# Start addresses of tiles: small tiles in a pool of their own, large tiles and rows on multiples of 64 bytes

## The chip, the cores and the metric

The kernel runs on one core of a Trainium2 chip. The metric is the device time of one execution in microseconds (us), as the median of several runs. The profile shows one execution, taken with the hardware profiler.

The engines are called as in the profile: PE is the matmul engine, with PEld for its loading of weights; DVE does elementwise work and reductions; ACT does activations and copies; POOL and SP complete them. SP's queue issues nearly all transfers here.

## The reference

An encoder trunk of two layers over 256 tokens of width 1024, in float32. Each layer adds three branches to x; each branch is normalised and modulated by shift, scale and gate that come from a condition vector c.

```python
c_act = jax.nn.silu(c)
for i in range(DEPTH):                                   # DEPTH = 2
    mod = (c_act @ mod_w[i] + mod_b[i])[:, None, :]      # 1024 -> 9 * 1024
    sh0, sc0, g0, sh1, sc1, g1, sh2, sc2, g2 = jnp.split(mod, N_MOD, axis=-1)
    h = modulate(rms_norm(x, norm_g[i, 0]), sh0, sc0)
    x = x + 0.5 * g0 * swiglu(h, ffn_w_gu[i, 0], ffn_w_down[i, 0])
    h = modulate(rms_norm(x, norm_g[i, 1]), sh1, sc1)
    y = pool_mixer(h, ...) if i == 0 else diff_attention(h, ...)
    x = x + g1 * y
    h = modulate(rms_norm(x, norm_g[i, 2]), sh2, sc2)
    x = x + 0.5 * g2 * swiglu(h, ffn_w_gu[i, 1], ffn_w_down[i, 1])
return rms_norm(x, final_g)
```

`swiglu` is `(silu(h @ Wg) * (h @ Wu)) @ Wd` with an inner width of 2816. The pooling mixer subtracts each token from its window's mean and multiplies by four matrices of 256 x 256. The attention has 8 heads with two softmaxes each, of which one is subtracted from the other.

## The kernel before

The tokens lie along the free dimension: `xT`, the running x, is 128 partitions x 8 rows x 256 tokens. A matmul has 128 x 128 weights, and 256 tokens stream past them.

Float32 products are made of three matmuls of the single-pass type `float32r`. Each operand is split into `hi`, its rounded value, and `lo`, what is left; the product is hi*hi + hi*lo + lo*hi (`prod3`, lines 333 to 335; `mm_deferred`, lines 431 to 433, does the same for the columns that are not normalised yet). The activations have such pairs in `xh`/`xl` (x times its scale), `hh`/`hl` (normalised), and `ah`/`al`, the two halves of `ahl` (inner activations of the feed-forward, values and outputs of the attention).

All weights come as a stream of 312 units of 128 x 1024 or 128 x 768 values. `split_unit` (line 304) takes for each a tile `raw` of 5 buffers, issues its load on SP's queue (line 310), lets ACT round it into `hi` (line 313) and DVE subtract it into `lo` (line 314); those have 6 buffers each. `prefetch` keeps five units ahead of the matmuls. A unit is issued again only when its buffers are free, so the matmuls pull the stream along.

Beside it runs the modulation, c times `mod_w`: 144 loads of 128 x 1024 into `u` (6 buffers, SP's queue), each followed by one multiply with sum on DVE (line 272). A list (`UP`, `DOWN`) says in which part of which feed-forward each of these steps is done; `Background.tick` spreads them over the units.

The stages follow one another: feed-forward, pooling mixer, feed-forward, then in layer 1 feed-forward, attention (its steps in an order written out by hand, `SCHED`), feed-forward, and the final norm. A tile framework orders each engine's instructions by priority and sets the semaphores.

Tiles come from pools. A pool hands out places in the order in which its tags are first asked for, and rounds each place up to a multiple of 32 bytes of a partition; pools lie one behind the other in the order in which they are made: `cpool` (what stays), `rawp`, `hip`, `lop`, `tmp`. Of what stays, in order of place: `ident` and `ones` (512 bytes each), `eps1` (4 bytes), `xT`, `xh`, `xl`, `hh`, `hl`, `ahl`, `cact`, `vecT` (836 bytes), the two `mod` (288 bytes each), `acc`, and some twenty vectors of 4 to 64 bytes. In the built program `ident` begins at byte 16,512 of a partition, `xT` at 17,568, `xh` at 25,760, `hh` at 42,208, `ahl` at 58,592, `acc` at 109,184, the five `raw` from 110,752 on, the six `hi` from 131,232, the six `lo` from 155,808, `u` from 189,632, `t` from 214,208. A row of `xh` has 258 values, or 1,032 bytes: 256 tokens and two columns for the shift, which `shift_cols` (line 409) writes and `shift_of` (line 452) reads back from the product.

`tmp` holds the temporary tiles, large and small: `t`, `u`, `qk`, `pk`, `rope`, `o`, and the tags `tiny`, `tinyw`, `tinyv`, `warm`, `rstdc` of 4 to 16 bytes.

Of the kernel before, what the change touches and what calls it, by code (L numbers as in the profile page):

```python
# [11 lines left out]
F32 = mybir.dt.float32  # L12
F32R = mybir.dt.float32r
# [3 lines left out]
AX = mybir.AxisListType  # L17

P = 128
D = 1024  # L20
KD = D // P
T = 256
NT = T // P
DFF = 2816
KF = DFF // P
EPS = 1e-6
# [36 lines left out]
def weight_units():  # L63

    def block(name, lead, r0, r1, c0, c1):
        return name, (*lead, slice(r0, r1), slice(c0, c1))

    def halves(name, lead, c0):
        yield block(name, lead, 0, 512, c0, c0 + UW)
        yield block(name, lead, 512, 1024, c0, c0 + UW)  # L70

    def ffn(i, s):
        first = 0
        if (i, s) == (0, 0):
            first = EARLY
            for k in range(KD):
                for n in range(2):
                    yield block("ffn_w_gu", (i, s), k * P, (k + 1) * P, n * DFF, n * DFF + EARLY * UW)
        for j in range(first, KF // 2):
            for n in range(2):  # L80
                yield from halves("ffn_w_gu", (i, s), n * DFF + j * UW)
        for dp in range(D // UW):
            for k0, k1 in DOWN_K:
                yield block("ffn_w_down", (i, s), k0 * P, k1 * P, dp * UW, (dp + 1) * UW)

# [5 lines left out]
    for tok in SCHED.split():  # L91
        n, u = tok[0], int(tok[1])
        if n in "qkv":
            yield from halves("diff_w_qkv", (), "qkv".index(n) * D + u * UW)
        elif n in "AB":
# [5 lines left out]
def unit_shape(ix):  # L101

    return (ix[-2].stop - ix[-2].start) // P, ix[-1].stop - ix[-1].start

# [8 lines left out]
def lay_out(inputs):  # L113
# [4 lines left out]
    head = np.concatenate([np.arange(16, 64), np.arange(0, 16), np.arange(64, P)])  # L118
    order = np.concatenate([h * P + head for h in range(2 * HEADS)] + [np.arange(2 * D, 3 * D)])
    w["diff_w_qkv"] = w["diff_w_qkv"][:, order]  # L120
    w["pool_w"] = w["pool_w"].reshape(D, UW)
    w["k_pool"] = consts["k_pool"]
# [20 lines left out]
def trunk(ctx: ExitStack, tc: tile.TileContext, x, c, mod_w, small, weights, diff_lambda, k_rope, out):  # L143
# [3 lines left out]
    cpool = ctx.enter_context(tc.tile_pool(name="cpool", bufs=1))  # L147
    rawp = ctx.enter_context(tc.tile_pool(name="rawp", bufs=RAW_BUFS))
    hip = ctx.enter_context(tc.tile_pool(name="hip", bufs=SPLIT_BUFS))
    lop = ctx.enter_context(tc.tile_pool(name="lop", bufs=SPLIT_BUFS))  # L150
    tmp = ctx.enter_context(tc.tile_pool(name="tmp", bufs=2))
    ps = ctx.enter_context(tc.tile_pool(name="ps", bufs=4, space=bass.MemoryType.PSUM))

    uid = [0]

    def nm(s):
        uid[0] += 1
        return f"{s}_{uid[0]}"

    def const(shape, name, dt=F32):  # L160
        return cpool.tile(shape, dt, tag=name, name=name)

    def psum():
        return ps.tile([P, 512], F32, tag="mm", name=nm("mm"), bufs=4)
# [4 lines left out]
    def psmall():  # L169
        return ps.tile([P, 512], F32, tag="st", name=nm("st"), bufs=2)  # L170
# [2 lines left out]
        return tmp.tile([P, n], F32, tag=tag, name=nm(tag), bufs=bufs)  # L173

    def tiny(n, dt=F32, tag="tiny", bufs=8):
        return tmp.tile([P, n], dt, tag=tag, name=nm(tag), bufs=bufs)

    def tinyw(n, dt=F32):
        return tiny(n, dt, "tinyw", 8)

    def tinyv(n, dt=F32):
        return tiny(n, dt, "tinyv", 6)
# [5 lines left out]


    ident = const([P, P], "ident")  # L190
    make_identity(nc, ident)
    ones = const([P, P], "ones")
    V.memset(ones, 1.0)

    pt = psum()
    for _ in range(WARM):
        PE.matmul(pt[:, :P], ones, ones, start=True, stop=True)

    eps1 = const([P, 1], "eps1")
    V.memset(eps1, 1.0)  # L200

    xT = const([P, KD, T], "xT")
    xh = const([P, KD, T + 2], "xh", F32R)
    xl = const([P, KD, T], "xl", F32R)
    hh = const([P, KD, T], "hh", F32R)
    hl = const([P, KD, T], "hl", F32R)
# [3 lines left out]
    def warm(f, after):  # L210

        S.activation(tiny(1, tag="warm", bufs=1), after, f, scale=0.0, bias=eps1)


    cact = const([P, D], "cact")
    for half in range(2):
# [132 lines left out]
    def newton(y, y0, v, t):  # L349
        V.tensor_tensor(t, y0, y0, ALU.mult)  # L350
        V.scalar_tensor_tensor(t, t, -0.5, v, ALU.mult, ALU.mult)
        V.scalar_tensor_tensor(y, t, 1.5, y0, ALU.add, ALU.mult)
# [27 lines left out]
    def rstd_cols():  # L380

        pt = psmall()
        for q in range(NT):
            PE.matmul(pt[:, q:q + 1], acc[:, q * P:(q + 1) * P], ones[:, 0:1], start=True, stop=True)
        v = tiny(NT)
        V.tensor_scalar(v, pt[:, :NT], 1.0 / D, EPS, ALU.mult, ALU.add)
        y = tmp.tile([P, NT], F32, tag="rstdc", name=nm("rstdc"), bufs=2)
        y0 = tiny(NT)
        S.activation(y0, v, AF.Abs_reciprocal_sqrt)
        newton(y, y0, v, tiny(NT))  # L390
        return y
# [167 lines left out]
    def pool_mixer(nxt):  # L559
# [5 lines left out]
        S.activation(hh[:, :, 0:P], bb, AF.Copy)  # L565
        V.tensor_tensor(hl[:, :, 0:P], bb, hh[:, :, 0:P].bitcast(F32), ALU.subtract)
        rstd = rstd_cols()

        def group(pt, g, q, lh, ll):
# [358 lines left out]
```

## Time and profile before

| | |
|---|---|
| median of 3 runs | 938.18 us (938.16 to 942.18) |
| the profiled execution | 942.75 us, its span 940.9 us |
| mean granted clock of PE | 0.992 |
| matmuls in the span | 7532 |
| read from HBM | 234.86 MB, 251 GB/s over the span |

The profile lists for each engine its busy time; matmuls overlap one another, so the time that one of them costs is read from start to start, in the timeline or by the count in a stretch. The chain of work is followed back from the last instruction: at each step to what released it. "L333" is line 333 of the kernel. A group such as "L335 PE MATMUL mm<-hh,lo" names the tile that is written, then the streamed tile, then the weights; a number such as x992 is its count.

### The profile page before, as it was taken

To read this page: it belongs to the slowest core of one execution; us is meant where nothing else is said; L and a number is where in the kernel's file an instruction comes from. 1 tells how busy PE (TensorE), PEld (TensorE's weight loads), DVE (VectorE), ACT (ScalarE), POOL (GpSimd) and SP (SyncE) were. 2 spreads that over 40 slices of the span, in tenths; PEclk is the share of its full clock that TensorE was granted. 3 is DMA by queue.
4 is the path that set the end of the run, shared out by engine and by line. 5 is a ranking of instruction groups with operands and counts; after the bars stand their busy time and mean duration, and the time that the engine had idled before them with its cause. 6 is when DMAs were issued, how large, how long until landed. Compare 5 with 4: busy or idle time off the path is not lost.

```text
span 940.9 us, 18753 instructions
## 1 busy us (share of the span) xinstructions
PE 911.2 (97%) x7532; PEld 897.5 (95%) x7532; DVE 743.6 (79%) x1211; ACT 505.4 (54%) x771; POOL 0.7 (0%) x6
## 2 busy tenths in 40 slices
PE   7899999899999999999999999999999999999997
PEld 7898889798999999999999999999999999999996
DVE  5868888789999777887988888888888897666451
ACT  5564435445665445455654454557777765444541
POOL 0000000000000000000000000000000000000000
PEclk9999999999999999999999999999999999999998
DMA  8988999888659887898599888855546548655531
GB/s 339 355 301 304 317 335 357 298 313 285 245 192 324 288 282 265 299 317 285 179 356 324 311 304 306 264 194 162 158 132 224 185 154 277 193 182 181 169 122 45
DMA packets 68727, 238.18 MB, mean 253 GB/s; under 512 B 7968, under 2 KB 9248, under 8 KB 68640
## 3 DMA queue, kind: packets, MB, share of 16 engines
q1 hardware_dynamic: 68496, 236.88, 73.8%
q8 instruction: 59, 0.97, 0.4%
q14 instruction: 28, 0.23, 0.1%
q10 hardware_dynamic: 144, 0.11, 0.0%
HBM read 234.86 MB, written 1.05 MB: 251 GB/s over the span
## 4 chain that ended last, share of the span: by engine, by line
PE 72%; DMA 12%; DVE 8%; ACT 4%; issue 3%; SPq 1%; DVEq 0%; ACTq 0%
PE mm L333 18%; PE mm L335 18%; PE mm L334 17%; DMA raw<-in_weights_dram 10%; DVE u L272 3%; DVE lo L314 3%; PE hd L335 3%; PE hd L333 3%; PE hd L334 3%; ACT hi L313 2%; PE mm L431 2%; PE mm L433 2%; PE mm L432 2%; PE hd L644 1%; DMA u<-in_mod_w_dram 1%
## 5 line engine op out<-in xcount | busy, mean ns | idle before, releaser
L313 ACT ACTIVATE hi<-raw 128x1024 fp32r<-128x1024 f32 (+1 forms) x312 | 318.6, 1025 | 339.2 <-PE mm L334 170.0
L314 DVE TENSOR_TENSOR lo<-raw,hi 128x1024 fp32r<-128x1024 f32 (+1 forms) x312 | 366.6, 1181 | 139.7 <-ACT hi L313 137.5
L335 PE MATMUL mm<-hh,lo 128*128 128x256 f32 x992 | 276.6, 281 | 4.4 <-DVE lo L314 4.4
L333 PE MATMUL mm<-hh,hi 128*128 128x256 f32 x992 | 277.7, 281 | 0.1
L334 PE MATMUL mm<-hl,hi 128*128 128x256 f32 x992 | 276.7, 280 | 0.0
L335 PE MATMUL mm<-ahl,lo 128*128 128x256 f32 x768 | 215.1, 280 | 2.2 <-DVE lo L314 2.2
L333 PE MATMUL mm<-ahl,hi 128*128 128x256 f32 x768 | 215.1, 280 | 1.8 <-ACT hi L313 1.8
L334 PE MATMUL mm<-ahl,hi 128*128 128x256 f32 x768 | 214.7, 280 | 0.0
L335 PEld LDWEIGHTS mm<-hh,lo 128*128 128x128 f32 x992 | 185.5, 188 | 6.6 <-DVE lo L314 6.0
L333 PEld LDWEIGHTS mm<-hh,hi 128*128 128x128 f32 x992 | 186.6, 188 | 1.3 <-ACT hh L420 0.4
L334 PEld LDWEIGHTS mm<-hl,hi 128*128 128x128 f32 x992 | 186.6, 188 | 0.0
L272 DVE SCALAR_TENSOR_TENSOR u<-u,cact 128x1024 f32<-128x1024 f32 x144 | 173.9, 1218 | 0.2 <-DMA u<-in_mod_w_dram 0.2
L335 PEld LDWEIGHTS mm<-ahl,lo 128*128 128x128 f32 x768 | 144.1, 188 | 3.4 <-DVE lo L314 3.4
L333 PEld LDWEIGHTS mm<-ahl,hi 128*128 128x128 f32 x768 | 144.2, 188 | 2.5 <-ACT hi L313 2.2
L334 PEld LDWEIGHTS mm<-ahl,hi 128*128 128x128 f32 x768 | 144.2, 188 | 0.0
L333 PE MATMUL hd<-hh,hi 128*128 128x256 f32 x288 | 81.2, 282 | 5.9 <-ACT hi L313 5.9
L335 PE MATMUL hd<-hh,lo 128*128 128x256 f32 x288 | 81.6, 283 | 3.9 <-DVE lo L314 3.9
L334 PE MATMUL hd<-hl,hi 128*128 128x256 f32 x288 | 80.7, 280 | 0.0
L333 PEld LDWEIGHTS hd<-hh,hi 128*128 128x128 f32 x288 | 54.3, 189 | 6.5 <-ACT hi L313 6.5
L335 PEld LDWEIGHTS hd<-hh,lo 128*128 128x128 f32 x288 | 54.3, 188 | 5.2 <-DVE lo L314 5.1
L432 PE MATMUL mm<-xl,hi 128*128 128x256 f32 x208 | 58.8, 285 | 0.0
L433 PE MATMUL mm<-xh,lo 128*128 128x258 f32 x208 | 58.3, 282 | 0.0
(199 smaller groups left out, 1034.7 us busy)
## 6 DMA issues: line engine op xcount, KB each, us to landing
raw<-in_weights_dram SPq DMA_DIRECT2D x264, 512.0 KB, 4.6
u<-in_mod_w_dram SPq DMA_DIRECT2D x144, 512.0 KB, 5.5
raw<-in_weights_dram SPq DMA_DIRECT2D x48, 384.0 KB, 5.0
xT<-in_x_dram SPq DMA_DIRECT2D x2, 512.0 KB, 5.0
out_dram<-u SPq DMA_DIRECT2D x4, 256.0 KB, 2.5
cact<-in_c_dram SPq DMA_DIRECT2D x1, 512.0 KB, 7.1
pk<-qk SPq DMA_DIRECT2D x16, 32.0 KB, 2.9
qk<-pk SPq DMA_DIRECT2D x16, 32.0 KB, 2.0
```

The lines of the kernel that those rows point to most:

```text
L272: return V.scalar_tensor_tensor(raw, raw, 1.0, cact, ALU.mult, ALU.mult, accum_out=out)
L313: S.activation(hi[:, :w], raw[:, :w], AF.Copy)
L314: splits.append(V.tensor_tensor(lo[:, :w], raw[:, :w], hi[:, :w].bitcast(F32), ALU.subtract).ins)
L333: PE.matmul(o, lh, rh, start=start, stop=False, **kw)
L334: PE.matmul(o, lh, rl, start=False, stop=False, **kw)
L335: PE.matmul(o, ll, rh, start=False, stop=stop, **kw)
L431: PE.matmul(o[:, :T + 2], hi[:, kk, cs], xh[:, k, :], start=(k == 0), stop=False)
L432: PE.matmul(o[:, :T], hi[:, kk, cs], xl[:, k, :], start=False, stop=False)
L433: PE.matmul(o[:, :T + 2], lo[:, kk, cs], xh[:, k, :], start=False, stop=(k == KD - 1))
L644: PE.matmul(sc[c2][:, q * T:(q + 1) * T], l[pr, 0, qs], r[pr, 1, :], start=(n == 0), stop=(n == 2))
```

## The change

Tiles whose last dimension is not a multiple of 16 values (64 bytes) move from `cpool` into a new pool `small_p`, which lies behind `tmp`; so do the tags `tiny`, `tinyw`, `tinyv`, `warm` and `rstdc`, which were in `tmp`. They keep their tags and numbers of buffers. `xh` gets rows of 272 values, 1,088 bytes, of which the first 258 are used as before. All instructions stay what they were, with other addresses.

```diff
+LINE = 16
...
     tmp = ctx.enter_context(tc.tile_pool(name="tmp", bufs=2))
+    small_p = ctx.enter_context(tc.tile_pool(name="small_p", bufs=1))
...
     def const(shape, name, dt=F32):
-        return cpool.tile(shape, dt, tag=name, name=name)
+        return (cpool if shape[-1] % LINE == 0 else small_p).tile(shape, dt, tag=name, name=name)
...
     def tiny(n, dt=F32, tag="tiny", bufs=8):
-        return tmp.tile([P, n], dt, tag=tag, name=nm(tag), bufs=bufs)
+        return small_p.tile([P, n], dt, tag=tag, name=nm(tag), bufs=bufs)
...
-    xh = const([P, KD, T + 2], "xh", F32R)
+    xh = const([P, KD, T + LINE], "xh", F32R)[:, :, :T + 2]
...
-        y = tmp.tile([P, NT], F32, tag="rstdc", name=nm("rstdc"), bufs=2)
+        y = tiny(NT, F32, "rstdc", 2)
```

## The prediction

> **What bounds the kernel now.** I read the page first, then the waits, the chain of single stages, and a table of stages. From the page: the span, the busy row and the chain's shares by engine.
>
> ```profile
> span 940.9 us, 18753 instructions
> PE 911.2 (97%) x7532; PEld 897.5 (95%) x7532; DVE 743.6 (79%) x1211; ACT 505.4 (54%) x771; POOL 0.7 (0%) x6
> GB/s 339 355 301 304 317 335 357 298 313 285 245 192 324 288 282 265 299 317 285 179 356 324 311 304 306 264 194 162 158 132 224 185 154 277 193 182 181 169 122 45
> PE 72%; DMA 12%; DVE 8%; ACT 4%; issue 3%; SPq 1%; DVEq 0%; ACTq 0%
> ```
>
> A busy share of 97% says little for PE, since matmul ends are modelled. The chain of a stage says more: first 60 to 240 us, then 300 to 440, then 640 to 735.
>
> ```profile
> by line: DMA raw<-in_weights_dram 51.5%; DVE lo L314 10.8%; DVE u L272 9.8%; issue 9.0%; ACT hi L313 8.2%; PE mm L335 1.9%; PE mm L333 1.6%; PE mm L334 1.6%; SPq L264 1.1%; DVE acc L407 1.0%; DVE qk L504 0.9%; DVE xl L343 0.8%; PE st L384 0
> by line: PE mm L334 28.6%; PE mm L333 28.0%; PE mm L335 27.9%; PE hd L334 4.1%; PE hd L333 4.0%; PE hd L335 4.0%; PE mm L431 1.0%; PE mm L432 1.0%; PE mm L433 1.0%; PE st L377 0.5%
> by line: PE mm L333 19.7%; PE mm L335 17.7%; PE mm L334 17.6%; PE hd L644 11.2%; DMA qk<-pk 6.1%; PE st L694 4.2%; PE st L675 2.8%; issue 2.2%; ACT u L655 2.1%; ACT hi L313 1.8%; PE st L721 1.7%; ACT o L704 1.6%; ACT xh L339 1.5%; ACT o L70
> ```
>
> Up to 240 us the weights' transfers are the bound; from there it is PE, except around the attention heads, where PE has a bit over half. The waits from 240 us on agree: ACT waits for matmuls to free a `hi` buffer, hardly ever for a transfer.
>
> ```profile
> ACT hi L313 <- PE mm L334: 166.9, 117, 2.2
> ACT hi L313 <- DMA raw<-in_weights_dram: 3.7, 2, 2.8
> ```
>
> The stages (columns: stretch, length, then busy us and count of PE, weight loads, DVE, ACT, POOL, granted clock, DMA share, GB/s):
>
> ```profile
> 60.00:240.00 180.00, 168.35 (x1360) 163.78 (x1359) 151.39 (x222) 83.53 (x106) 0.00 (x0) 0.98 0.89 316
> 240.00:300.00 60.00, 59.42 (x498) 58.86 (x497) 59.04 (x110) 38.09 (x61) 0.00 (x0) 1.00 0.75 259
> 300.00:440.00 140.00, 140.00 (x1186) 139.73 (x1185) 108.10 (x152) 68.13 (x86) 0.00 (x0) 1.00 0.87 296
> 440.00:480.00 40.00, 39.99 (x337) 39.79 (x336) 38.09 (x74) 26.58 (x38) 0.00 (x0) 1.00 0.68 219
> 480.00:600.00 120.00, 120.00 (x1021) 120.00 (x1020) 99.44 (x139) 57.19 (x69) 0.00 (x0) 1.00 0.91 319
> 600.00:640.00 40.00, 40.00 (x336) 39.76 (x335) 32.21 (x56) 21.25 (x30) 0.00 (x0) 1.00 0.62 195
> 640.00:735.00 95.00, 94.11 (x773) 89.25 (x772) 82.53 (x203) 72.65 (x183) 0.00 (x0) 1.00 0.55 175
> 735.00:780.00 45.00, 44.91 (x373) 44.41 (x372) 42.45 (x86) 32.17 (x52) 0.00 (x0) 1.00 0.51 164
> 780.00:925.00 145.00, 145.00 (x1232) 144.84 (x1232) 84.43 (x98) 66.84 (x83) 0.00 (x0) 1.00 0.55 175
> ```
>
> So the question is what one matmul of 256 columns costs. In the last stage it is 145 us / 1,230 = 117.9 ns from start to start (two of the 1,232 stick out of the window). The timeline of PE gives the same: first and last of 13 rows, 1.41 us / 12 = 117.5.
>
> ```profile
> 349.73 0.28 PE L335 MATMUL mm<-hh,lo 128*128 128x256 f32 x1
> ...
> 351.14 0.28 PE L335 MATMUL mm<-hh,lo 128*128 128x256 f32 x1
> ```
>
> At half the clock it is not proportionally longer. Here are the stretch 235 to 239 us (PE, clock 0.50) and the first and last of seven rows in it: 1.28 us / 6 = 213.3 ns, or 0.833 ns a column.
>
> ```profile
> 235.00:239.00 4.00, 4.00 (x21) 0.50 0.46 133
> 235.69 0.41 PE L335 MATMUL mm<-hi,xl 128*128 128x256 f32 x1
> ...
> 236.97 0.42 PE L335 MATMUL mm<-hi,xl 128*128 128x256 f32 x1
> ```
>
> At the full clock a column should then take 0.417 ns and 256 columns 106.7. The matmuls take 11 ns more, and this excess is the only thing on the path that the change can reach.
>
> **The change part by part.** No instruction is added or removed: the same tags with the same buffers are taken from another pool, so engine order, DMAs and waits stay. What changes is addresses. In `cpool`, `eps1` (4 bytes, in a slot of 32) puts all that follows at 32 past a multiple of 64: `xT` lies at byte 17,568 of a partition, `hh` at 42,208, `ahl` at 58,592, `raw` from 110,752, `hi` and `lo` behind it. Tiles of `tmp` (`t`, `u`, `qk`), `ones`, `acc` lie on multiples of 64 already. Rows of `xh` are 1,032 bytes apart and become 1,088. By my reckoning of the pools in order `xT` goes to 17,536, `raw` to 109,184, and every large tile to a multiple of 64.
>
> *DVE and ACT.* The trace has the same operation on tiles at both places. Of DVE, `acc<-acc,t` lies wholly on multiples of 64, `ahl<-t,ahl` only in its `t`. Of ACT, `xT<-xT` lies wholly off them, `qk<-t` wholly on them (the vectors of scales are a few bytes).
>
> ```profile
> L407 DVE TENSOR_TENSOR acc<-acc,t 128x256 f32<-128x256 f32 x41 | 17.2, 419 | 0.8 <-ACT t L406 0.5
> L340 DVE TENSOR_TENSOR ahl<-t,ahl 128x256 fp32r<-128x256 f32 x12 | 4.9, 419 | 0.4 <-ACT ahl L339 0.3
> L894 ACT ACTIVATE xT<-xT,vecT 128x256 f32<-128x256 f32 x7 | 3.2, 496 | 0.0
> L748 ACT ACTIVATE qk<-t,tiny 128x256 f32<-128x256 f32 x8 | 3.7, 504 | 1.0 <-DVE tiny L746 1.0
> ```
>
> 419 against 419 ns on DVE. On ACT 496 off and 504 on (L748 also adds a bias). I take nothing; bounds: 8 ns either way on some 700 ACT instructions, none of them in the chain of 300 to 440 us.
>
> *Transfers.* `u` already lands on multiples of 64, `raw` does not; the issues (KB, us to landing) show no gain for `u`, so I take nothing for the first 240 us.
>
> ```profile
> raw<-in_weights_dram SPq DMA_DIRECT2D x264, 512.0 KB, 4.6
> u<-in_mod_w_dram SPq DMA_DIRECT2D x144, 512.0 KB, 5.5
> ```
>
> *PE.* Every large matmul streams a row of 1,024 bytes from an odd multiple of 32, with weights from one too. 64 bytes are 16 columns, 6.67 ns at the full clock. Such a row touches 17 pieces of 64 bytes, an aligned one 16. In one stretch of the attention stage the same kind of matmul runs in another rhythm: first and last of 15 rows, 1.59 us / 14 = 113.6 ns.
>
> ```profile
> 700.23 0.28 PE L333 MATMUL mm<-hi,hh 128*128 128x256 f32 x1
> ...
> 701.82 0.28 PE L335 MATMUL mm<-hi,hl 128*128 128x256 f32 x1
> ```
>
> 17 pieces would be 113.3. The usual 117.8 is 53 pieces for three matmuls (117.78), as if two in three had one piece more to wait for. Both fit whole pieces of 64 bytes, which is why I believe that the start matters. That is an inference: no row shows a large single-pass matmul with both operands aligned. The nearest aligned rows are fp32 ones, which by their times take two passes:
>
> ```profile
> 7.18 2.54 PE L814 MATMUL st<-u,ones 128*128 128x256 f32 x11
> 10.21 2.73 PE L817 MATMUL st<-ones 128*128 128x128 f32 x23
> 933.20 0.30 PEld L882 LDWEIGHTS st<-ones,pk 128*128 128x128 f32 x2
> 933.42 0.30 PEld L881 LDWEIGHTS st<-ones,acc 128*128 128x128 f32 x2
> 933.64 0.30 PEld L882 LDWEIGHTS st<-ones,pk 128*128 128x128 f32 x2
> ```
>
> L814 streams aligned rows: its last matmul lasts 0.38, so ten starts take 2.54 - 0.38 = 2.16 us, 216 ns for two passes, only 2.7 over 2 x 106.7. An aligned pass has next to no excess. L817 has half the columns (106.7 in two passes) and takes (2.73 - 0.28) / 22 = 111.4; L881 and L882 stream one column, and four weight loads take 0.44 us, 110. So a weight load needs 110 to 112 ns, more than 256 aligned columns, and sets the new floor. Ends: 109.4 (aligned stream alone) and 117.8 (nothing changes); above that, the slow rival. I take 111.6, a gain of 6.2 ns, as L817 has both at work.
>
> The Trainium skill, page "TensorE: Matmul & The Clock Gate", section "Wait — 56ns, not 53.3ns?", gives N / 2.4 GHz plus about 2.5 ns between warm matmuls, thus an estimate of 109.2 ns for 256 columns; L814 agrees, the large matmuls here do not, and by it alone the sum below would be that of rival two.
>
> **Sum**, stage by stage, count x 6.2 ns, then what is left of it:
> - 240 to 300: 3.1 us; DVE is busy 59.0 of 60 and becomes the bound: 1.0.
> - 300 to 440: 7.4; 296 GB/s becomes 312, about what the first stage holds (316): 6.0.
> - 440 to 480: 2.1; DVE is at 38.1 of 40: 1.5.
> - 480 to 600: 6.3; 319 GB/s would become 336, above the 316 of the transfer-bound stage and below single slices of 355 to 357: 4.5.
> - 600 to 640: 2.1, all.
> - 640 to 735: 4.8; lines 333 to 335 carry 55% of that chain: 2.6.
> - 735 to 780: 2.3; DVE at 42.5 of 45: 1.8.
> - 780 to 925: 7.6, all: transfers are at 175 GB/s, DVE at 58%.
>
> Together 27.1 of 35.7 us. The profiled execution took 942.75 us (span 940.9), 0.5% over the median of 938.18 of three runs; taken off either, it gives 915.6 and 911.1. I forecast 911.
>
> **The rivals.**
> - *Two, the weight load is not the floor:* 109.4 ns, 8.4 off each. The same table gives 48 us raw, but the caps on DVE and transfers stay: about 36, thus 902. For it: L814. Against: L817 and L881.
> - *Three, only the stumble goes:* 113.3 ns remain as a fixed cost, 4.5 off; 26 raw, about 20 kept, 918. For it: the stretch at 700 us reaches 113 unaligned.
> - *Four, no change:* the excess belongs to the single-pass format, reading four bytes for each column at full clock, and starts on 32 are good enough; or a tile doesn't land where I reckon. 938. For it: two rhythms at one alignment, so something besides the start decides.
>   The Trainium skill, page "SBUF — State Buffer", section "Specifications (TRN2)", gives lines of 16 bytes, to which all these rows already begin aligned but for half of those of `xh`; by that rule the time stays at 938. No row here tells 16 from 64 for a 1,024-byte row, while the steps of 6.67 ns speak for 64.
> - *Five, slower:* now `hh` and `ahl` begin 64 bytes away from `hi` and `lo` modulo 128; afterwards all begin at 0. If load and stream then meet in the same piece each time, one more piece per matmul costs 6.67 ns x 5,800 = 39 us: 977. It decides once intervals pass 117.8. Against: in L817 load and stream read the very same tile at 111.4.
>
> **How the numbers follow.** Forecast 0.45, two 0.15, three 0.15, four 0.16, five 0.09. About 0.5% (4.7 us) is what a measurement can tell from no change; so faster 0.75, same 0.16, slower 0.09. The likeliest case's own range is 903 to 920 (its caps wholly absent, or the attention and DMA-heavy stages giving nothing). The range over the cases goes from 896 (rival two with half its caps) to 940 (no change).
>
> **What would show it.** Right: a stretch near the end with DVE and DMA idle shows 111 to 112 ns a matmul; the end of the transfer-bound part stays near 240 us; ACT waits less for L334 and more for `raw`; DVE is full after each residual. Wrong: 117.8 ns again (four), 113.3 (three), or more than 118 (five); or 111.6 but with PE idle behind `lo` or `raw` from 300 to 600 us, which would put the time near 920.

## The result and the profile after

The changed kernel takes 949.45 us (median of 5 runs, 946.22 to 950.84); beside it the kernel before took 938.18 (5 runs, 937.48 to 942.18). The ratio is 1.0103, 95% interval 1.0075 to 1.0132: slower by about 1%, outside the predicted range and on the other side of no change. The profiled execution took 950.84 us.

The page of the changed kernel, its span, busy row and the chain's shares by engine (line numbers are up to three higher than before):

```profile
span 949.1 us, 18753 instructions
PE 923.8 (97%) x7532; PEld 911.9 (96%) x7532; DVE 743.3 (78%) x1211; ACT 505.8 (53%) x771; POOL 0.7 (0%) x6
PE 74%; DMA 11%; DVE 8%; ACT 3%; issue 3%; SPq 1%; DVEq 0%; ACTq 0%
```

The counts are the same and the busy times of DVE and ACT have hardly moved. PE is busy for 12.6 us more, and its share of the chain rose from 72 to 74%. The stages show it without doubt; these are four of the stretches shown of before, with the same columns (stretch, length, busy us and count of PE, weight loads, DVE, ACT, POOL, clock, DMA share, GB/s):

```profile
60.00:240.00 180.00, 172.41 (x1378) 168.97 (x1376) 153.24 (x227) 85.40 (x108) 0.00 (x0) 0.98 0.89 318
300.00:440.00 140.00, 139.99 (x1165) 139.73 (x1165) 106.27 (x148) 66.78 (x83) 0.00 (x0) 1.00 0.85 291
480.00:600.00 120.00, 120.00 (x1003) 120.00 (x1002) 97.31 (x135) 56.88 (x69) 0.00 (x0) 1.00 0.90 312
780.00:925.00 145.00, 145.00 (x1210) 145.00 (x1210) 87.54 (x100) 68.13 (x84) 0.00 (x0) 1.00 0.57 185
```

In the last three PE is full in both kernels, at full clock, and issues fewer matmuls: 1165 for 1186, 1003 for 1021, 1210 for 1232, or 1.8% fewer each time. The first stretch, where the transfers are the bound, lost nothing (1378 for 1360). So each matmul has become longer from start to start, and the timeline of PE says by how much: first and last of 13 rows, 1.44 us / 12 = 120.0 ns, where it was 117.5 to 117.9.

```profile
349.74 0.28 PE L337 MATMUL mm<-hl,hi 128*128 128x256 f32 x1
...
351.18 0.28 PE L337 MATMUL mm<-hl,hi 128*128 128x256 f32 x1
```

Over the prediction's 5,800 matmuls 2.2 ns are 12.8 us; the medians moved by 11.3. Nothing else moved: the split's subtraction on DVE takes 1181 ns in both kernels, transfers land 0.1 to 0.2 us sooner, and ACT waits for the matmuls to free `hi` a little longer (175.0 us from 240 us on, before 166.9). These are a row of the groups, two of the DMA issues, and one of the waits, of the changed kernel:

```profile
L317 DVE TENSOR_TENSOR lo<-raw,hi 128x1024 fp32r<-128x1024 f32 (+1 forms) x312 | 366.7, 1181 | 146.8 <-ACT hi L316 144.2
raw<-in_weights_dram SPq DMA_DIRECT2D x264, 512.0 KB, 4.5
u<-in_mod_w_dram SPq DMA_DIRECT2D x144, 512.0 KB, 5.3
ACT hi L316 <- PE mm L337: 175.0, 118, 2.2
```

So the whole effect is in the interval of the matmuls, and the question is what sets it: where a tile starts, or how far the weights start from the stream.

### The profile page after: what moved, and what is told of

It is laid out like the page before. It is cut to its first block, busy times and chain, and to the rows that moved or that the text cites. A ratio compares the mean times of both kernels' runs of the same rounds, so it can differ in the third digit from the quotient of the medians.

```text
span 949.1 us, 18753 instructions
## 1 busy us (share of the span) xinstructions
PE 923.8 (97%) x7532; PEld 911.9 (96%) x7532; DVE 743.3 (78%) x1211; ACT 505.8 (53%) x771; POOL 0.7 (0%) x6
## 4 chain that ended last, share of the span: by engine, by line
PE 74%; DMA 11%; DVE 8%; ACT 3%; issue 3%; SPq 1%; DVEq 0%; ACTq 0%
PE mm L336 18%; PE mm L338 18%; PE mm L337 18%; DMA raw<-in_weights_dram 9%; DVE u L275 4%; DVE lo L317 3%; PE hd L338 3%; PE hd L337 3%; PE hd L336 3%; PE mm L434 2%; PE mm L435 2%; PE mm L436 2%; ACT hi L316 2%; PE hd L647 1%; DMA u<-in_mod_w_dram 1%
## 5 line engine op out<-in xcount | busy, mean ns | idle before, releaser
L316 ACT ACTIVATE hi<-raw 128x1024 fp32r<-128x1024 f32 (+1 forms) x312 | 318.3, 1025 | 345.4 <-PE mm L337 175.0
L317 DVE TENSOR_TENSOR lo<-raw,hi 128x1024 fp32r<-128x1024 f32 (+1 forms) x312 | 366.7, 1181 | 146.8 <-ACT hi L316 144.2
L336 PE MATMUL mm<-hh,hi 128*128 128x256 f32 x992 | 281.3, 285 | 0.0
L338 PE MATMUL mm<-hh,lo 128*128 128x256 f32 x992 | 279.9, 285 | 1.3 <-DVE lo L317 1.2
L337 PE MATMUL mm<-hl,hi 128*128 128x256 f32 x992 | 280.5, 284 | 0.0
L338 PE MATMUL mm<-ahl,lo 128*128 128x256 f32 x768 | 219.5, 286 | 3.0 <-DVE lo L317 3.0
L336 PE MATMUL mm<-ahl,hi 128*128 128x256 f32 x768 | 219.5, 286 | 1.1 <-ACT hi L316 1.1
L337 PE MATMUL mm<-ahl,hi 128*128 128x256 f32 x768 | 219.2, 285 | 0.0
L338 PEld LDWEIGHTS mm<-hh,lo 128*128 128x128 f32 x992 | 189.4, 192 | 2.7 <-DVE lo L317 2.1
L336 PEld LDWEIGHTS mm<-hh,hi 128*128 128x128 f32 x992 | 190.7, 192 | 0.8
L337 PEld LDWEIGHTS mm<-hl,hi 128*128 128x128 f32 x992 | 190.6, 192 | 0.0
L338 PEld LDWEIGHTS mm<-ahl,lo 128*128 128x128 f32 x768 | 148.6, 193 | 3.8 <-DVE lo L317 3.8
L336 PEld LDWEIGHTS mm<-ahl,hi 128*128 128x128 f32 x768 | 148.6, 194 | 1.7 <-ACT hi L316 1.3
L337 PEld LDWEIGHTS mm<-ahl,hi 128*128 128x128 f32 x768 | 148.7, 194 | 0.0
```

Source lines behind the costliest of these rows:

```text
L316: S.activation(hi[:, :w], raw[:, :w], AF.Copy)
L317: splits.append(V.tensor_tensor(lo[:, :w], raw[:, :w], hi[:, :w].bitcast(F32), ALU.subtract).ins)
L336: PE.matmul(o, lh, rh, start=start, stop=False, **kw)
L337: PE.matmul(o, lh, rl, start=False, stop=False, **kw)
L338: PE.matmul(o, ll, rh, start=False, stop=stop, **kw)
```

## The experiments

"Distance" below is the start of the weights minus the start of the stream, both as bytes within a partition, modulo 256. By the pools' order it was 192 before the change (streams `hh`, `hl`, `xl`, `ahl` start at 224 modulo 256, `hi` and `lo` at 160), and is 0 after it (both at 128). Two theories: **places** (the start of each tile by itself sets the interval; in the expectations theory S for the stream's start and W for the weights') and **distance** (theory R). Theory E is the traffic of the other engines.

**The matmul by itself.** Bursts of 192 matmuls, 128 x 128 weights of float32r, new ones for each, with the starts chosen by hand:

```diff
+    for i in range(192):
+        PE.matmul(o[:, :256], wr(96, i), xr(32, i, 256), **flags(i))  # stream 32, weights 96, 256 columns
```

> The kernel leaves out all of the trunk: it runs only bursts of 192 float32r matmuls in the trunk's order (hi with hh, hi with hl, lo with hh), one line of code for each pair of starts (bytes past a multiple of 512 of the streamed row and of the weights), with no other engine busy; then six of them again behind four transposes. The trunk showed 117.8 ns a matmul at stream 96, weights 32 (mod 128) and 120.0 at 0, 0. Theory S (the start of the stream alone decides): 120.0 wherever the stream begins at 0, 64 or 128, 117.8 wherever at 32 or 96, whatever the weights. Theory W (the start of the weights alone decides): 120.0 with weights at 0, 64, 128, 256; 117.8 with 32 or 96. Theory R (what counts is the distance between the two, as the load of the next weights meets the stream): 0,0 and 32,32 and 16,16 alike at 120.0, 96,32 and 32,96 and 0,64 and 64,0 alike at 117.8. Theory E (it is other engines' traffic, not the starts): all cases alike. With 512 columns, twice 106.7 plus the excess: if a stream pays for each straddled piece, 213.3 at start 0 and 220 at 32; if the load of weights is what costs, the same for both. With 128 and 64 columns the load alone sets the time, 111 to 112 at 0 by the rows of before.

The timeline of PE in this run; each row is one burst (start us, length us, count), in the order stream/weights 0/0, 32/32, 96/32, 32/96, then 16/16; then with 512 columns 0/0, 32/0, 32/32; then 128 columns:

```profile
12.96 23.28 PE L68 MATMUL mm<-xs,ws 128*128 128x256 f32 x192
36.08 23.19 PE L72 MATMUL mm<-xs,ws 128*128 128x256 f32 x192
59.11 22.78 PE L76 MATMUL mm<-xs,ws 128*128 128x256 f32 x192
81.72 21.93 PE L80 MATMUL mm<-xs,ws 128*128 128x256 f32 x192
...
193.84 22.57 PE L100 MATMUL mm<-xs,ws 128*128 128x256 f32 x192
...
375.52 43.71 PE L132 MATMUL mm<-xs,ws 128*128 128x512 f32 x192
419.07 44.97 PE L136 MATMUL mm<-xs,ws 128*128 128x512 f32 x192
508.66 43.71 PE L144 MATMUL mm<-xs,ws 128*128 128x512 f32 x192
552.22 21.55 PE L148 MATMUL mm<-xs,ws 128*128 128x128 f32 x192
```

A burst's length less its last matmul (0.28 us), over 191, is the interval: 120.4 ns for 0/0, then 119.9, 117.8 and 113.4. From 32/32 to 32/96 all start at odd multiples of 32, and the interval still takes three values. 0/0 settles at 120.0 as 32/32 does; only its first matmuls were slower. So being on a multiple of 64 gains nothing, and with no other engine at work both intervals of the two kernels come back at their distances: 117.8 at 192, 120.0 at 0.

Not every pair follows its distance, though. 16/16 was expected at 120.0 as well and takes (22.57 - 0.28) / 191 = 116.7. 0/64 was expected at 117.8 and took that, but 32/96, at the same distance, took 113.4. In the burst of 64 columns the granted clock fell to 0.50, so it tells nothing of the load.

With 512 columns, too, 0/0 equals 32/32, and 32/0 takes 1.26 us / 191 = 6.6 ns more; 0/32, where the stream is the aligned one, takes 6.5 more. A cost for straddled pieces of the stream would differ between aligned and unaligned rows; this one does not. The excess over the columns' own time (0.417 ns each) at distance 0 is 13.3 ns for 256 columns and, with 226.7 from start to start, 226.7 - 213.3 = 13.4 for 512, so at this distance it does not grow with the row. At 32/0 it does, from 116.6 - 106.7 = 9.9 to 233.3 - 213.3 = 20.0. With 128 columns the burst shows the weight load: (21.55 - 0.22) / 191 = 111.7 ns.

**All distances.** The same loop in bursts of 48, stream at 0, weights at 0 to 496 in steps of 16, each burst once behind a wait and once behind a chain of transposes (the cut shows as one line what the kernel has once for each pair):

```diff
-        PE.matmul(o[:, :256], wr(96, i), xr(32, i, 256), **flags(i))
+        PE.matmul(o[:, :256], wr(d, i), xr(s, i, 256), **flags(i))   # d = 0, 16, ... 496
```

> Leaves out the trunk, as the first such kernel: bursts of 48 float32r matmuls, stream at 0 and weights at 0, 16, ... 496 bytes past a multiple of 512, each once behind a wait for ACT and once behind four transposes; then six pairs with the stream at 32 and the trunk's own pair of before (224, 160). Theory R (the distance weights minus stream decides): the pairs at 32 repeat those at 0 with the same distance; distance 0 and 256 give 120.0 ns, and some distances give 113.3 or less. Theory S (the stream's start decides) has by now one row against it (32, 32 gave 120.0 in the first such kernel); it would have the whole list at 120. The pair of before should give 117.8 or 113.3, by its history.

From the timeline of PE, bursts at stream 0 and weights 64, 192, 224, 256, 320; then stream/weights 32/32, 32/96 and the old kernel's 224/160:

```profile
63.10 5.60 PE L116 MATMUL mm<-xs,ws 128*128 128x256 f32 x48
161.24 5.81 PE L196 MATMUL mm<-xs,ws 128*128 128x256 f32 x48
185.59 5.76 PE L216 MATMUL mm<-xs,ws 128*128 128x256 f32 x48
209.90 5.91 PE L236 MATMUL mm<-xs,ws 128*128 128x256 f32 x48
259.16 5.62 PE L276 MATMUL mm<-xs,ws 128*128 128x256 f32 x48
406.28 5.91 PE L396 MATMUL mm<-xs,ws 128*128 128x256 f32 x48
430.99 5.60 PE L416 MATMUL mm<-xs,ws 128*128 128x256 f32 x48
479.80 5.82 PE L456 MATMUL mm<-xs,ws 128*128 128x256 f32 x48
```

Less 0.28 and over 47: 113.2, 117.7, 116.6, 119.8, 113.6, 119.8, 113.2, 117.9 ns. The pattern repeats with 256 bytes (256 as 0, 320 as 64). At distances 0, 32, 64 and 224 the pairs with the stream at 32 repeat those with the stream at 0 within 0.3 ns, and so does 224/160 at 192; 32/160 does not quite, with 120.0 where 0/128 takes 118.7. All 16 distances in steps of 16, by the mean from start to start: 0: 120.0 (the first bursts, with some slower starts, 121.7); 16: 118.4; 32: 118.3; 48: 117.8; **64: 113.3**; 80 and 96: 118.7; 112: 120.0; 128: 118.7; 144: 118.4; 160: 119.9; 176: 118.1; 192: 117.8; 208 and 224: 116.7; 240: 117.3. Only one stands out, and the change went to one of the worst.

**Places held, distance changed; distance held, places changed.** Six kernels of the whole trunk. A small pool ahead of `hi` and `lo` pushes both along; 16 values are 64 bytes:

```diff
     rawp = ...
+    shiftp = ctx.enter_context(tc.tile_pool(name="shiftp", bufs=1))
     hip = ...
...
+    V.memset(shiftp.tile([P, 16], F32, tag="shift", name="shift"), 0.0)
```

- `e1_near`: before, with 16 values. All large tiles stay at odd multiples of 32; distance 0.

> The kernel before with a pad of 64 bytes ahead of hi and lo, nothing else: every large tile still lies at an odd multiple of 32, but weights and streams now begin at the same place modulo 512 (224 and 224). Theory R (distance): 120.0 ns a matmul, near 949 us as after the change. Theory S or W (multiples of 64 as such cost): 117.8 ns, 938 us.

- `e2_rows_only`: before, with only the rows of `xh` longer; distance 192.

> The kernel before with rows of xh of 1088 bytes alone: tiles stay at odd multiples of 32, and streams stay 64 bytes from the weights modulo 512. Theory R: 117.8 ns and 938 us, within 0.5%. If the padding of xh itself were what costs (two of three matmuls in the deferred units read it): 949 us, with a longer interval in L431 and L433 alone.

- `e3_after_ahead`: after, with 16 values. All large tiles stay at multiples of 64; distance 64.

> The changed kernel with a pad of 64 bytes ahead of hi and lo: all large tiles stay on multiples of 64, but weights now begin 64 bytes after the stream modulo 256. Theory R with the list of distances (64 gave 113.3 behind a wait and behind transposes, 117.8 in a chain that ran at that before): 113.3 ns for most matmuls after 240 us, so 6.7 ns off 120.0 for 5,800 of them, 39 us raw, less what DVE and transfers take back: 915 to 925 us. If the matmuls fall into the other rhythm: 117.8 ns, 938. Theory S or W (multiples of 64 are what costs): 120.0 ns, 949.

- `e4_before_ahead`: before, with 32 values. Odd multiples of 32; distance 64.

> The kernel before with a pad of 128 bytes ahead of hi and lo: all large tiles stay at odd multiples of 32; weights begin 64 bytes after the stream modulo 256, where before they began 64 bytes before it. Theory R: as the run with the changed kernel and 64 bytes, 113.3 ns and 915 to 925 us. If multiples of 64 matter beside the distance, it is slower than that run by over 0.5%.

- `e5_pool_only`: after, with the rows of `xh` back at 1,032 bytes; distance 0.

> One part of the change alone: small tiles in their own pool, rows of xh 1,032 bytes as before. Large tiles lie on multiples of 64, weights and streams (hh, hl, xl, ahl) at the same place modulo 256. Theory R: 120.0 ns, 946 to 950 us; all of the loss is in this part. If the rows of xh carry the loss: 938.

- `e6_pool_behind`: that, with 48 values. Multiples of 64; distance 192.

> The run with the pool alone, and a pad of 192 bytes ahead of hi and lo: tiles on multiples of 64, weights 64 bytes before the stream modulo 256, the distance of the kernel before. Theory R: 117.8 ns, 936 to 941 us, as before. Theory S or W: 120.0 ns, 949.

| kernel | places | distance | median us (range) | ratio to before (95%) |
|---|---|---|---|---|
| e1 | odd 32s | 0 | 947.27 (945.09 to 948.28) | 1.0112 (1.0049 to 1.0175) |
| e5 | 64s | 0 | 949.52 (948.12 to 950.47) | 1.0117 (1.0087 to 1.0146) |
| e2 | odd 32s | 192 | 940.70 (935.07 to 944.53) | 1.0040 (1.0003 to 1.0077) |
| e6 | 64s | 192 | 938.04 (935.69 to 941.39) | 0.9996 (0.9977 to 1.0015) |
| e4 | odd 32s | 64 | 928.34 (926.88 to 936.75) | 0.9922 (0.9877 to 0.9967) |
| e3 | 64s | 64 | 928.22 (918.28 to 938.25) | 0.9911 (0.9863 to 0.9959) |

The kernels pair off by distance: with either kind of place the time is near 948, 939 or 928. The stretch 300 to 420 us of e1, e2, e3, e5 and e6, in that order, has the columns of the stages above; the count of PE is what to read:

```profile
300.00:420.00 120.00, 120.00 (x1002) 120.00 (x1001) 91.20 (x125) 56.77 (x71) 0.00 (x0) 1.00 0.84 284
```

```profile
300.00:420.00 120.00, 120.00 (x1021) 120.00 (x1021) 91.70 (x125) 56.84 (x69) 0.00 (x0) 1.00 0.85 293
```

```profile
300.00:420.00 120.00, 120.00 (x1061) 120.00 (x1060) 96.17 (x134) 59.86 (x74) 0.00 (x0) 1.00 0.88 303
```

```profile
300.00:420.00 120.00, 120.00 (x1002) 120.00 (x1001) 90.24 (x121) 56.17 (x68) 0.00 (x0) 1.00 0.85 287
```

```profile
300.00:420.00 120.00, 120.00 (x1021) 120.00 (x1021) 93.22 (x128) 57.86 (x73) 0.00 (x0) 1.00 0.85 290
```

Two of each count stick out of the window; 120 us over the rest gives 120.0, 117.8, 113.3, 120.0 and 117.8 ns. The places theory falls: e1 leaves every place as bad as it was by that theory and loses the full 1.1%, e6 puts every place right and gains nothing. The pool alone (e5) makes the whole loss. The longer rows of `xh` alone (e2) leave the interval at 117.8; its ratio's interval only just excludes 1, too little to build on.

e3 and e4 gained less than the interval should give, and spread widely. The same stretch and the last feed-forward of e4 show what happened in one execution:

```profile
300.00:420.00 120.00, 120.00 (x1062) 120.00 (x1061) 97.63 (x138) 60.33 (x74) 0.00 (x0) 1.00 0.88 305
780.00:900.00 120.00, 120.00 (x1021) 120.00 (x1020) 69.65 (x77) 56.63 (x68) 0.00 (x0) 1.00 0.53 172
```

113.2 ns first and 117.8 in the end, in one execution, with the same tiles and distance. Distance 64 has two rhythms in the kernel, 113.3 and 117.8. The execution of e3 with the profile held 113.3 nearly throughout and took 918.28 us, the lowest of its six. The slower executions have no profile, so that they spent more time at 117.8 is not shown.

The kernel before has both rhythms too. In three longer stretches of the attention the roles are swapped: `hi` and `lo` stream, and `hh` and `hl` are the weights, so that the distance is 224 - 160 = 64. One of them is the stretch at 700 us which the prediction read at 113.6 ns. The one at 674 us has the same distance and runs at 117.7 (first and last of 14 rows, 1.53 us / 13):

```profile
674.43 0.28 PE L333 MATMUL mm<-hi,hh 128*128 128x256 f32 x1
...
675.96 0.28 PE L334 MATMUL mm<-lo,hh 128*128 128x256 f32 x1
```

The third, at 649 us, takes 117.6. After the change the distance is 0 in either role, and all three take 119.9 to 120.0.

**Finer steps, and a distance of its own for each kind of weights.** Of three matmuls two use `hi` and one uses `lo`, so the two may lie apart. Bursts of 48 behind a wait, bursts of 72 behind a chain of matmuls at distance 192 (again in short form):

```diff
-        PE.matmul(o[:, :256], wr(d, i), xr(s, i, 256), **flags(i))
+        PE.matmul(o[:, :256], wr(dl if i % 3 == 2 else dh, i), xr(0, i, 256), **flags(i))   # dh for hi, dl for lo
```

> Leaves out the trunk: bursts with the stream at 0 and weights at finer distances (4 to 248 bytes), then pairs of different distances for hi and lo; each burst once behind a wait, and once directly behind 24 matmuls that run at distance 192 in the rhythm of 117.8 ns. Theory R, with a rhythm that persists: distance 64 gives 113.3 behind the wait and 117.8 behind the chain. Its rival (the distance alone sets the interval, what came before does not): the same value in both, 113.3. A distance that gives under 114 in both would be the better place for the weights. In the order hi with hh, hi with hl, lo with hh, a load of lo runs beside the stream of hl and two loads of hi beside hh: if the loads' distances count one by one, hi 64 with lo elsewhere gives a third of the way to the other value.

From the timeline of PE: distance 76 behind a wait and behind the chain; then, behind the chain, `hi` at 64 with `lo` at 192, and `hi` at 192 with `lo` at 64:

```profile
209.48 5.92 PE L200 MATMUL mm<-xs,ws 128*128 128x256 f32 x48
218.07 8.35 PE L206 MATMUL mm<-xs,ws 128*128 128x256 f32 x72
...
449.75 8.32 PE L349 MATMUL mm<-xs,ws 128*128 128x256 f32 x72
467.36 8.72 PE L360 MATMUL mm<-xs,ws 128*128 128x256 f32 x72
```

Distance 76 takes (5.92 - 0.28) / 47 = 120.0 ns behind a wait and (8.35 - 0.28) / 71 = 113.7 behind the chain: what ran before can decide. At 64 it was 113.3 in both places, where 117.8 was expected behind the chain. But that chain did not run at 117.8, as the one ahead of 76 did. These are the burst at 64, the chain behind it and the second burst at 64; last, the chain ahead of 76:

```profile
156.34 5.62 PE L167 MATMUL mm<-xs,ws 128*128 128x256 f32 x48
161.80 2.88 PE L170 MATMUL mm<-xs,ws 128*128 128x256 f32 x24
164.52 8.32 PE L173 MATMUL mm<-xs,ws 128*128 128x256 f32 x72
...
215.24 2.99 PE L203 MATMUL mm<-xs,ws 128*128 128x256 f32 x24
```

(2.88 - 0.28) / 23 is 113.0 ns, (2.99 - 0.28) / 23 is 117.8, both at distance 192. So this run does not answer whether the rhythm of 117.8 persists at 64, and it shows something else: 192, the distance of the kernel before, has the two rhythms of 64. The chain ran at 113 in 7 of 34 places, four of them behind bursts at 113.3, the others not. The first run of bursts had shown both at 64: 0/64 took 117.8 ns in its place in the row of bursts and settled at 113.3 behind transposes. Around 64 the picture is ragged: 52 and 88 settle at 113.3, but 56, 60, 68 and 72 give 117.8 to 119.5. And mixed distances don't average: `hi` 64 with `lo` 192 gives 113.2 (two thirds of 113.3 and one of 117.8 would be 114.8; the chain ahead of it ran at 113 as well), the reverse 118.9 (for 116.3).

**The two mixed layouts in the kernel.** Both on e5's base, with one pad ahead of `hi` and one between `hi` and `lo`; e7 has `hi` at distance 64 and `lo` at 192, e8 the reverse.

```diff
+    V.memset(shiftp.tile([P, 16], F32, tag="shift", name="shift"), 0.0)     # e8: 48 values
+    V.memset(shiftq.tile([P, 32], F32, tag="shift2", name="shift2"), 0.0)   # between hi and lo
```

> The run with the pool alone, with pads of 64 bytes ahead of hi and 128 more ahead of lo: hi begins 64 bytes after the stream modulo 256, lo 192. The bursts with this pair gave 113.3 ns behind a wait and behind a chain alike. Theory R with loads that count one by one: 113.3 ns in most stretches, 915 to 930 us, and a smaller spread than the run with 64 for both if this pair holds its rhythm better. Its rival (the two distances average out between 113.3 and 117.8): 116.3 ns, 930 to 935.

> The same with the distances swapped: hi 192 bytes after the stream, lo 64. The bursts gave 118.9 ns. Theory R, loads one by one: 118.9 ns, 1.1 ns over before for 5,800 matmuls after 240 us, so 6 us more, 942 to 947. Rival (average): as the run before it.

e7: 924.82 us (920.90 to 925.43), ratio 0.9856 (0.9797 to 0.9915). e8: 935.21 (928.87 to 939.43), ratio 0.9961 (0.9925 to 0.9996). The stages of e7, an early, a middle and a late stretch:

```profile
300.00:420.00 120.00, 120.00 (x1061) 120.00 (x1060) 95.91 (x133) 59.91 (x75) 0.00 (x0) 1.00 0.88 305
440.00:480.00 40.00, 39.88 (x344) 39.69 (x343) 39.52 (x72) 25.14 (x36) 0.00 (x0) 1.00 0.69 245
780.00:900.00 120.00, 120.00 (x1062) 120.00 (x1061) 72.82 (x83) 59.07 (x72) 0.00 (x0) 1.00 0.57 178
```

and two of e8:

```profile
300.00:420.00 120.00, 120.00 (x1062) 120.00 (x1061) 96.98 (x135) 59.26 (x74) 0.00 (x0) 1.00 0.88 307
780.00:900.00 120.00, 120.00 (x1011) 120.00 (x1010) 70.86 (x80) 56.40 (x68) 0.00 (x0) 1.00 0.58 181
```

e7 holds 113.3 in both long stretches, and its four runs lie within 4.5 us; it is 1.4% faster than the kernel before that ran beside it, at the same number of matmuls. e8 was expected at 942 to 947 and is not: in the early stretch it runs at 113.2 ns, in the late one at 120 / 1,009 = 118.9. Here, too, one layout has two rhythms in the kernel, and the bursts had shown only the worse one.

**What stays open.** That the distance, and not the place, makes the difference between the two kernels is shown from both sides, for tiles that start on multiples of 32. The distance alone does not fix the interval: 64 and 192 have been seen at 113.3 and at 117.8, e8 at 113.3 and 118.9, while at 0 such tiles always settled at 120.0. What picks between two rhythms is not shown, nor is what collides in the memory or in PE, nor why 16/16 departs from 0/0. Four runs do not make sure that e7 always stays in the good rhythm.

## Why the prediction was wrong

*Where the bound is:* right. From 300 to 440 us PE is full in both kernels (140.0 of 140 us), and only the interval of its matmuls moved; the transfer-bound part up to 240 us lost nothing.

*DVE, ACT and transfers cost nothing:* right. DVE's and ACT's busy times moved by 0.3 and 0.4 us in all, and transfers by 0.1 to 0.2 us each.

*The excess comes from straddled pieces of 64 bytes, so alignment takes it away:* this step failed. It took 6.2 ns off each matmul, and 2.2 were added. It rested on intervals that happen to be whole pieces (53 for three matmuls, 17 for one). The row of the 17 pieces, at 700 us, was not the usual matmul in another rhythm: its streams and weights are swapped, and its distance is 64 where the usual one is 192. The bursts give 120.0 ns for aligned rows at 0/0, the same as at 32/32; the excess belongs to the pair of weights and stream. Whole pieces were not a proof either: 116.6 and 118.3 to 118.7 occur just as well.

*"An aligned pass has next to no excess", and the load floor of 111.6:* the rows were read rightly but could not answer the question. L814's pass over 256 columns is made twice for one product, so 216 ns leave its load twice the time; L817 is bound by its load. The burst of 128 columns shows the latter: 111.7 ns at 0/0 and at 32/32 alike, at a distance that costs 13.3 ns with 256 columns. The lowest interval at which any layout settled here with 256 columns is 113.3, 1.6 above the load's own. None reached the 109.4 of rival two, and so it is out. The Trainium skill's estimate from "TensorE: Matmul & The Clock Gate", section "Wait — 56ns, not 53.3ns?", 109.2 ns, was not reached by any of them either.

*Rival five* had the right quantity and the wrong price. It named the distance between load and stream, and that it would be 0 afterwards (modulo 128, where the bursts repeat with 256); it charged one more piece, 6.67 ns, where 2.2 were measured, and came to 977 instead of 949. Its term was mis-sized because it took pieces as the unit; whether load and stream meet as it supposed is not shown. What spoke against it, L817, was the load-bound row that could show no collision at all.

*Rival four* would have left the time at 938. The runs differ: e5 and e7, whose large tiles all begin at multiples of 16 with the same half of the rows of `xh` off them, lie 24.7 us apart by their medians. So the lines of 16 bytes of the Trainium skill's page "SBUF — State Buffer", section "Specifications (TRN2)", do not tell these layouts apart.

*The stage table* can be tested at 113.3 ns, since e7 reaches it. Rival three kept 20 of 26 us; e7 gained 13.9 by the medians. The best execution of e3, at 918.28, lies just where that rival put the time, but partly by luck: from 60 to 240 us, where the transfers are the bound, it got through 1401 matmuls, against 1360 before and 1365 in e7. The cap on DVE after the residual was right: in 440 to 480 us of e7 DVE is busy 39.5 of 40 us, with 344 matmuls instead of 337.

## What to carry to other kernels

Where matmuls follow each other with new weights each time, a PE that is 97% busy can still have something to gain, here 117.8 ns a matmul against 113.3 in another layout: take the interval from start to start, compare it with the columns' time and with the load alone, and then try the start of the weights against the start of the stream, at a cost of some bytes of padding. Aligning everything is no aim in itself; here it moved the pair from a middling distance to a bad one. A row used as the nearest example has to be bound by the same thing as the work that it stands for; a burst of 48 matmuls per candidate answers in one run what the trace of the kernel could not, though not which of two rhythms the kernel will keep.

## What the runs showed of the hardware that was not expected

- The interval of float32r matmuls with 128 x 128 new weights and 256 columns depends on the distance of weights and stream modulo 256 bytes: in the long stretches of the kernels 113.3 or 117.8 ns at 64, 117.8 at 192, 120.0 at 0. Where the pair lies matters little for starts on multiples of 32: the same distance gave the same interval within 1.3 ns, apart from the two rhythms. It held less well for other starts: 16/16 took 116.7 where 0/0 takes 120.0.
- At distance 0 the excess is 13.3 ns for 256 columns and 13.4 for 512; at distance 224 (32/0) it is 9.9 and 20.0.
- Some layouts have two rhythms: distance 64 and distance 192 were both seen at 113 and at 117.8 ns. What ran before can choose: at distance 76, 120.0 ns behind a wait and 113.7 behind a chain.
- A mixed layout is not the mean of its parts: 113.2 and 118.9 ns, where means would be 114.8 and 116.3.
